# Query blocks first to last in a fused decoder trunk on one core

## The chip, the core and the metric

The kernel runs on one core of a Trainium2 chip, in one launch. The time is the device time of the whole program in microseconds (us), from the first to the last instruction with a little around it. A core has five engines, each with its own queue that it works through in order: TensorE (matmuls, PE in the profile, its weight loads PEld), VectorE (DVE), ScalarE (ACT), GpSimd (POOL) and SyncE (SP, which here only issues DMAs). They wait for each other by semaphores. Matmuls write to PSUM, eight banks of 128 partitions by 512 fp32 words.

## The reference

Two layers over 512 tokens of width 1024 in fp32. Each is a SwiGLU, a mixing part and a second SwiGLU, all with residuals. The mixing part, cut to what matters:

```python
h = rms_norm(x, mix_norm[l])
a, g, q, k, v = jnp.split(h @ w_in[l], splits, axis=-1)
conv_out = conv_module(a, g, conv_w[l], conv_b[l], conv_norm[l])      # 512 channels, 31 causal taps
...
def block(args):                       # 128 queries, 4 heads, 2 maps each, causal
    qi, i = args
    s = jnp.einsum("bhmqd,bhmkd->bhmqk", qi, k) * scale + bias[None, :, None]
    s = jnp.where((dist >= 0)[None, None, None], s, -1e30)
    p = jax.nn.softmax(s, axis=-1)
    a = p[:, :, 0] - lam * p[:, :, 1]
    return jnp.einsum("bhqk,bhkd->bhqd", a, v)
...
o = rms_norm(o, subln_g) * (1.0 - lam_init)
x = x + jnp.concatenate([conv_out, diff_out], axis=-1) @ w_out[l]
```

Query block i of four sees the keys of blocks 0 to i alone. The result of one block does not depend on another's, and the output projection adds up its two halves per token, so both may be taken in any order.

## The kernel before

Features lie on partitions and tokens along the row: `x`, and its split into a high part and a rest (`acth`, `actl`), are eight tiles of 128 x 512. To keep fp32 precision with faster matmuls most products are three: high by high, high by rest, rest by high (`mm3`, L200, L203, L204). Weights are split in the same way when they arrive (`parts_of`: ScalarE copies at L101, VectorE or GpSimd subtracts at L102). `chunk` loads two tiles of 128 x 512 from a ring of five and splits them.

The kernel is a Python program that emits instructions for a scheduler. The scheduler puts every engine's queue in an order of its own, from priorities in the program's order and its estimate of durations; where buffers are shared it adds semaphore waits. So a change of the program's order changes queues on all engines.

`mixer` does one mixing part. First come the projections: convolution inputs (`conv_in`, gate at L785 to L791 on VectorE), queries and keys (`project`, `to_features`), and four value tiles (`project_values`, L843 to L845: 24 matmuls of 512 columns each, evacuated by ScalarE at L846). They keep TensorE full while VectorE and GpSimd already do convolution taps: channel tile 0 is wholly on GpSimd (31 taps), 1 and 2 on VectorE, 3 shared (10 taps on GpSimd, L885, fed by ScalarE at L884; the other 21 on VectorE, L895 and L899, joined at L902).

Attention runs in 16 steps, a query block i with a head h. A step has two score maps of 128 x W, W = 128 (i + 1):

- `softmaxes`: two score matmuls (L930, fp32) into a bank of tag "sc" and one of tag "po", two banks each; for each map VectorE adds the bias and takes the row's minimum (L934; scores are negated), ScalarE the exponential with its sum (L938), the first map from an SBUF tile that L934 writes, the second in its bank; then VectorE inverts the sum (L941), scales it (L943) and joins both maps (L944). The "sc" bank is free after L934, the "po" bank after L944.
- `keys_first`, two steps later: i + 1 transposes of the joined map into the one bank "tp" (L951) and ScalarE's copy (L953).
- `values`, three steps later: i + 1 products with the values (L960) into a bank `ps_o`. After the last head of a block its norm follows: square on ScalarE (L969), sum on VectorE (L971), GpSimd adds and takes the inverse root (L972, L261 as `rs_y`), VectorE scales (L975).
- `block_out`, five steps later: four transposes (L987) and the split of the result (L989 on ScalarE, L990 on VectorE) into `acth`, `actl`.

`conv_finish` sums the squares of the convolution per token (TensorE transposes, L268; VectorE L272, L273; GpSimd `rs_y`; VectorE L288; TensorE `ps_spread`, L292; ScalarE L296), then scales and activates the four channel tiles (GpSimd L910, ScalarE L912, VectorE L913, ScalarE L914, VectorE L915).

The output projection makes three passes over eight feature tiles: the attention half of two query blocks (256 columns, 96 matmuls), the convolution half of all tokens (512 columns, 96 matmuls), the attention half of the other two blocks. Each pass loads and splits its weights again, on ScalarE and GpSimd. Its banks are "sc" and "po" again; VectorE adds each result to `x` (L1037), and in the last pass `after(m)` begins the preparation of the next SwiGLU.

Before, attention takes query block 3 first and block 0 last, and values are projected for tokens 384 to 511 first. The first pass of the output projection is that of tokens 256 to 511.

Of the kernel before, what the change touches and what calls it, by code (L numbers as in the profile page):

```python
# [20 lines left out]
SEQ = 512  # L21
DM = 1024
KT = DM // P
NT = SEQ // P
# [7 lines left out]
HEADS = 4  # L32
# [38 lines left out]
def trunk(ctx: ExitStack, tc: tile.TileContext, xt, par, lamv, relb, onehot,  # L71
# [17 lines left out]
    def bank(tag, name):  # L89
        return psum.tile([P, 512], F32, tag=tag, name=name, bufs=BANKS[tag])  # L90
# [14 lines left out]
    def chunk(src, eng=None):  # L105
        w = []
        for n in range(2):
            raw = ring("wraw")
            nc.sync.dma_start(raw, src[:, n * 512 : (n + 1) * 512])
            w.append(parts_of(raw, eng))  # L110
        return w

    def wpart(w, b, n=P):
        hi, lo = w[b * n // 512]
        c = b * n % 512
        return hi[:, c : c + n], lo[:, c : c + n]
# [81 lines left out]
    def mm3(ps, w, x, start, stop, pin=False):  # L198
        (wh, wl), (xh, xl) = w, x
        first = T.matmul(ps, wh, xh, start=start, stop=False)  # L200
        if pin:
            tc.keep_in_program_order(first)
        T.matmul(ps, wh, xl, start=False, stop=False)  # L203
        T.matmul(ps, wl, xh, start=False, stop=stop)  # L204
# [553 lines left out]
    def mixer(l, pr, after, begun):  # L758
        with tc.tile_pool(name="mix", bufs=1) as mp, tc.tile_pool(name="mt", bufs=2) as mt:
# [74 lines left out]
            def project_values(j):  # L834

                if 2 not in wts:
                    wts[2] = [chunk(wqkv[l, 2, kc], G) for kc in range(KT // 2)]
                t = slice(j * P, (j + 1) * P)
                ps = bank("mm", "ps_v")
                for k in range(KT):  # L840
                    wh, wl = wpart(wts[2][k // 2], k % 2, 512)
                    xh, xl = pr[k]
                    T.matmul(ps, xh[:, t], wh, start=k == 0, stop=False)  # L843
                    T.matmul(ps, xh[:, t], wl, start=False, stop=False)  # L844
                    T.matmul(ps, xl[:, t], wh, start=False, stop=k == KT - 1)  # L845
                S.activation(vv[:, j].rearrange("p h d -> p (h d)"), ps, AF.Copy, scale=row["c"][:, j : j + 1])  # L846
# [68 lines left out]
                    V.scalar_tensor_tensor(cl[:, c, :], z, hg, f32(ch[:, c, :]), op0=ALU.mult, op1=ALU.subtract)  # L915


            steps = [(i, h) for i in reversed(range(NT)) for h in range(HEADS)]
            sums, pos, maps, ats = {}, {}, {}, {}

            def softmaxes(i, h):
# [72 lines left out]
            def attend(n):  # L994
                if n < len(steps):
                    softmaxes(*steps[n])
                if 2 <= n < len(steps) + 2:
                    keys_first(*steps[n - 2])
                if 3 <= n < len(steps) + 3:
                    values(*steps[n - 3])  # L1000
                if n >= 5 and steps[n - 5][1] == HEADS - 1:
                    block_out(steps[n - 5][0])
# [12 lines left out]

            for n in range(2):
                attend(n)
                project_values(NT - 1 - 2 * n)
                project_values(NT - 2 - 2 * n)
            for c in range(CT):  # L1020
                conv_taps(c, POOL_TAPS[c])
            for n in range(2, len(steps) + 5):
                attend(n)
            conv_finish()

            for half, t in ((1, slice(SEQ // 2, SEQ)), (0, slice(0, SEQ)), (1, slice(0, SEQ // 2))):
                w = [None] * 4
                for m in range(KT):  # L1030
                    if w[m // 2] is None:
                        w[m // 2] = chunk(wout[l, half, m // 2], G)
                    ps = bank(("sc", "po")[m % 2], "ps_out")[:, : t.stop - t.start]
                    for kk in range(4):
                        k = half * 4 + kk
                        mm3(ps, wpart(w[m // 2], (m % 2) * 4 + kk), (ch[:, k, t], cl[:, k, t]), kk == 0, kk == 3)
                    V.tensor_tensor(x[:, m, t], ps, x[:, m, t], op=ALU.add)  # L1037

                    if half == 1 and t.start == 0 and m < KT // 2:
                        after(m)  # L1040
            for m in range(KT // 2, KT):
                after(m)
# [16 lines left out]
    for l in range(DEPTH):  # L1059
        nxt = {}  # L1060

        def preparing(gain, l2=l):
            def after(m):
                if m == 0:
                    nxt["p"] = Prep(l2, gain)
                nxt["p"].tile(m)
            return after

        def store(m):
            nc.sync.dma_start(out[m], x[:, m, :])  # L1070

        with tc.tile_pool(name="ffn", bufs=1) as fp:
            begun = ffn(fp, pr, gu1[l], dn1[l], preparing("mix_norm"), begun,
                        lambda tail: begin(nxt["p"], [[wag[l, c, i] for i in range(2)] for c in range(2)], tail),
                        (l == 0, 1), aside if l == 0 else None)
        mixer(l, nxt["p"], preparing("ffn2_norm"), begun)
        with tc.tile_pool(name="ffn", bufs=1) as fp:
            begun = begin(nxt["p"], [[gu2[l, m, i] for i in range(2)] for m in range(2)])
            if l + 1 < DEPTH:
                begun = ffn(fp, nxt["p"], gu2[l], dn2[l], preparing("ffn1_norm", l + 1), begun,  # L1080
                            lambda tail: begin(nxt["p"], [[gu1[l + 1, m, i] for i in range(2)] for m in range(2)], tail), (0, 1))
            else:
                ffn(fp, nxt["p"], gu2[l], dn2[l], store, begun, lambda tail: tail(), (0, 0))
        pr = nxt["p"]
# [74 lines left out]
```

## Time and profile before

| what | value |
|---|---|
| time, median of 3 runs | 1771.87 us (1771.71 to 1772.9) |
| time of the profiled execution | 1772.54 us |
| its span, first to last instruction | 1770.8 us |
| TensorE busy | 1759.9 us, 99% |
| weight loads busy | 1621.3 us, 92% |
| VectorE / ScalarE / GpSimd busy | 1470.9 / 1039.5 / 515.1 us |
| granted TensorE clock, mean | 1.000 |
| score matmuls, first to last in the program | 453.3 to 1379.1 us |

The profile is that of one execution. Where a row of a timeline reads `453.48 3.60 PE L930 MATMUL ps_sc<-kt,qz ... x8`, eight records of line 930 on TensorE begin at 453.48 us and take 3.60 us; the tile written stands left of the arrow, those read right of it. A group's row gives the count, the busy time with the mean duration of one in nanoseconds, and the idle time of the engine just before the group's instructions with what ended it. A window's row gives, for each engine, busy us and instructions in brackets, then the granted clock, the share of the DMA engines and GB/s. Matmuls overlap one another, so a busy TensorE is not one at its peak; the distance between the starts says more than the durations.

### The profile page before, as it was taken

To read this page: it belongs to the slowest core of one execution; us is meant where nothing else is said; L and a number is where in the kernel's file an instruction comes from. 1 tells how busy PE (TensorE), PEld (TensorE's weight loads), DVE (VectorE), ACT (ScalarE), POOL (GpSimd) and SP (SyncE) were. 2 spreads that over 40 slices of the span, in tenths; PEclk is the share of its full clock that TensorE was granted. 3 is DMA by queue.
4 is the path that set the end of the run, shared out by engine and by line. 5 is a ranking of instruction groups with operands and counts; after the bars stand their busy time and mean duration, and the time that the engine had idled before them with its cause. 6 is when DMAs were issued, how large, how long until landed. Compare 5 with 4: busy or idle time off the path is not lost.

```text
span 1770.8 us, 32986 instructions
## 1 busy us (share of the span) xinstructions
PE 1759.9 (99%) x11853; PEld 1621.3 (92%) x11853; DVE 1470.9 (83%) x2642; ACT 1039.5 (59%) x1951; POOL 515.1 (29%) x497
## 2 busy tenths in 40 slices
PE   9999999999999999999999999999999999999998
PEld 7799999988788899999988999999887888999998
DVE  7969888969877969889987798899698678698987
ACT  6546566755865436566644565666559554465664
POOL 1011112169970011112200121121798600111122
PEclk9999999999999999999999999999999999999999
DMA  7457677533223457687544577766231335577774
GB/s 222 135 135 184 166 197 190 135 122 96 71 78 113 123 130 178 172 198 177 143 144 108 149 176 180 194 161 177 81 113 48 101 105 134 133 184 173 194 176 126
DMA packets 165894, 257.79 MB, mean 146 GB/s; under 512 B 19191, under 2 KB 61958, under 8 KB 165728
## 3 DMA queue, kind: packets, MB, share of 16 engines
q1 hardware_dynamic: 129024, 201.38, 36.7%
q0 software_dynamic: 36416, 54.12, 19.0%
q8 instruction: 93, 1.52, 0.3%
q14 instruction: 73, 0.60, 0.1%
q10 hardware_dynamic: 288, 0.16, 0.0%
HBM read 253.48 MB, written 3.42 MB: 145 GB/s over the span
## 4 chain that ended last, share of the span: by engine, by line
PE 95%; DVE 2%; DMA 1%; POOL 1%; ACT 1%; issue 0%; SPq 0%; ACTq 0%; DVEq 0%; POOLq 0%
PE ps_pair L435 36%; PE ps_pair L524 17%; PE ps_pair L203 9%; PE ps_pair L204 9%; PE ps_pair L200 9%; PE ps_out L200 2%; PE ps_out L203 2%; PE ps_out L204 2%; PE ps_pair L815 2%; PE ps_pair L814 2%; PE ps_pair L813 2%; PE ps_sc L930 1%; PE ps_v L844 1%; PE ps_v L843 1%; PE ps_v L845 1%; POOL wlo L102 0%
## 5 line engine op out<-in xcount | busy, mean ns | idle before, releaser
L101 ACT ACTIVATE whi<-wraw 128x512 fp32r<-128x512 f32 x744 | 454.0, 628 | 421.9 <-PE ps_pair L203 174.8
L102 DVE TENSOR_TENSOR wlo<-wraw,whi 128x512 fp32r<-128x512 f32 x640 | 427.0, 685 | 116.7 <-ACT whi L101 105.2
L160 POOL DMA_DIRECT2D wsum<-in_gu x128 | 112.2, 907 | 703.7 <-DMA wsum<-in_gu 276.0
L435 PE MATMUL ps_pair<-acth,wlo 128*128 128x256 f32 x1024 | 289.8, 283 | 0.0
L435 PE MATMUL ps_pair<-actl,whi 128*128 128x256 f32 x1024 | 289.8, 283 | 0.0
L435 PE MATMUL ps_pair<-acth,whi 128*128 128x256 f32 x1024 | 289.8, 283 | 0.0
L435 PE MATMUL ps_pair<-th,whi 128*128 128x256 f32 x768 | 217.3, 283 | 0.0
L435 PE MATMUL ps_pair<-tl,whi 128*128 128x256 f32 x768 | 217.3, 283 | 0.0
L435 PE MATMUL ps_pair<-th,wlo 128*128 128x256 f32 x768 | 217.3, 283 | 0.0
L200 PE MATMUL ps_pair<-acth,whi 128*128 128x512 f32 x512 | 199.4, 394 | 0.5 <-ACT acth L309 0.4
L203 PE MATMUL ps_pair<-actl,whi 128*128 128x512 f32 x512 | 199.5, 390 | 0.3 <-DVE actl L310 0.3
L204 PE MATMUL ps_pair<-acth,wlo 128*128 128x512 f32 x512 | 199.2, 390 | 0.0
L435 PEld LDWEIGHTS ps_pair<-actl,whi 128*128 128x128 f32 x1024 | 196.6, 192 | 0.2
L435 PEld LDWEIGHTS ps_pair<-acth,whi 128*128 128x128 f32 x1024 | 196.6, 192 | 0.2
L435 PEld LDWEIGHTS ps_pair<-acth,wlo 128*128 128x128 f32 x1024 | 196.6, 192 | 0.0
L160 POOL DMA_DIRECT2D wsum<-in_dn x112 | 98.8, 1132 | 266.6 <-DMA wsum<-in_dn 45.6
L435 PEld LDWEIGHTS ps_pair<-th,whi 128*128 128x128 f32 x768 | 147.5, 192 | 0.0
L435 PEld LDWEIGHTS ps_pair<-tl,whi 128*128 128x128 f32 x768 | 147.5, 192 | 0.0
L435 PEld LDWEIGHTS ps_pair<-th,wlo 128*128 128x128 f32 x768 | 147.5, 192 | 0.0
L102 POOL TENSOR_TENSOR wlo<-wraw,whi 128x512 fp32r<-128x512 f32 x104 | 137.1, 1339 | 31.8 <-ACT whi L101 19.5
L524 PE MATMUL ps_pair<-hh,whi 128*128 128x256 f32 x512 | 144.9, 283 | 0.0
L524 PE MATMUL ps_pair<-hl,whi 128*128 128x256 f32 x512 | 144.9, 283 | 0.0
(207 smaller groups left out, 4445.2 us busy)
## 6 DMA issues: line engine op xcount, KB each, us to landing
wraw<-in_gu SPq DMA_DIRECT2D x284, 256.0 KB, 3.5
wsum<-in_gu SPq DMA_DIRECT2D x128, 256.0 KB, 3.8
wsum<-in_gu POOLq DMA_DIRECT2D x128, 256.0 KB, 4.7
wraw<-in_dn SPq DMA_DIRECT2D x68, 256.0 KB, 3.3
wraw<-in_wqkv SPq DMA_DIRECT2D x48, 256.0 KB, 2.9
wraw<-in_wout SPq DMA_DIRECT2D x48, 256.0 KB, 3.0
wraw<-in_dn SPq DMA_DIRECT2D x64, 128.0 KB, 4.2
wraw<-in_wag SPq DMA_DIRECT2D x32, 256.0 KB, 3.0
```

Source lines behind the costliest of these rows:

```text
L101: S.activation(hi, raw, AF.Copy)
L102: (eng or V).tensor_tensor(out=lo, in0=raw, in1=f32(hi), op=ALU.subtract)
L160: nc.gpsimd.dma_start(dst[:, to], src, accum_op=ALU.add)
L200: first = T.matmul(ps, wh, xh, start=start, stop=False)
L203: T.matmul(ps, wh, xl, start=False, stop=False)
L204: T.matmul(ps, wl, xh, start=False, stop=stop)
L435: mm = T.matmul(ps, l, r, start=first and i == j == 0, stop=False, skip_group_check=True)
L524: mm = T.matmul(ps, s[:, f], r, start=side not in self.begun, stop=False, skip_group_check=True)
L813: T.matmul(ps[n], xh[:, t], wh, start=k == 0, stop=False)
L814: T.matmul(ps[n], xh[:, t], wl, start=False, stop=False)
L815: T.matmul(ps[n], xl[:, t], wh, start=False, stop=k == KT - 1)
L843: T.matmul(ps, xh[:, t], wh, start=k == 0, stop=False)
```

## The change

Attention's 16 steps are listed with block 0 first. The value tiles follow the same order: tokens 0 to 127 first, two tiles behind each of the first two steps. The first pass of the output projection is the attention half of tokens 0 to 255, the third that of tokens 256 to 511; the next part's preparation stays with the third pass.

```diff
-            steps = [(i, h) for i in reversed(range(NT)) for h in range(HEADS)]
+            steps = [(i, h) for i in range(NT) for h in range(HEADS)]
...
             for n in range(2):
                 attend(n)
-                project_values(NT - 1 - 2 * n)
-                project_values(NT - 2 - 2 * n)
+                project_values(2 * n)
+                project_values(2 * n + 1)
...
-            for half, t in ((1, slice(SEQ // 2, SEQ)), (0, slice(0, SEQ)), (1, slice(0, SEQ // 2))):
+            for half, t in ((1, slice(0, SEQ // 2)), (0, slice(0, SEQ)), (1, slice(SEQ // 2, SEQ))):
...
-                    if half == 1 and t.start == 0 and m < KT // 2:
+                    if half == 1 and t.stop == SEQ and m < KT // 2:
                         after(m)
```

## The prediction

> **What bounds the kernel now.** I read the page's chain of waits first, then windows of the mixers, the timelines of TensorE and VectorE in the first attention, and the groups by shape there.
>
> ```profile
> PE 95%; DVE 2%; DMA 1%; POOL 1%; ACT 1%; issue 0%; SPq 0%; ACTq 0%; DVEq 0%; POOLq 0%
> ```
>
> TensorE sets the time: 95% of the chain that ended last is its own work. The change adds and removes no matmul, so it can only alter how long TensorE stands still in the two mixers. The windows cut the first mixer where the last value projection is issued (467.80) and where the conv statistics begin (492.66).
>
> ```profile
> core 0: us, PE busy (x) PEld busy (x) DVE busy (x) ACT busy (x) POOL busy (x), PEclk, DMA share, GB/s
> 467.80:492.66 24.86, 24.42 (x144) 18.44 (x143) 21.61 (x75) 24.12 (x68) 21.12 (x19) 1.00 0.29 85
> 492.66:506.66 14.00, 13.33 (x105) 12.20 (x104) 12.80 (x48) 11.01 (x34) 9.01 (x9) 1.00 0.01 2
> 506.66:520.00 13.34, 13.34 (x83) 11.88 (x82) 8.89 (x13) 7.67 (x14) 13.26 (x11) 1.00 0.48 142
> 1345.40:1370.10 24.70, 24.28 (x143) 18.27 (x142) 21.42 (x74) 23.94 (x68) 20.97 (x19) 1.00 0.29 86
> ```
>
> TensorE is nearly full here; ScalarE (24.12 of 24.86) and VectorE (21.61) have little room. Mixer 2 repeats mixer 1. What TensorE does per map comes from start times, since its durations overlap:
>
> ```profile
> 453.48 3.60 PE L930 MATMUL ps_sc<-kt,qz 128*128 128x512 f32 x8
> ...
> 467.80 1.88 PE L930 MATMUL ps_sc<-kt,qz 128*128 128x512 f32 x4
> 469.52 0.60 PE L951 MATMUL ps_at<-ident,e 128*128 128x128 f32 x4
> 469.95 2.53 PE L930 MATMUL ps_sc<-kt,qz 128*128 128x512 f32 x6
> ...
> 472.75 1.06 PE L960 MATMUL ps_o<-vv,at 128*128 128x128 f32 x8
> 473.65 2.75 PE L930 MATMUL ps_sc<-kt,qz 128*128 128x384 f32 x8
> 476.23 0.60 PE L951 MATMUL ps_at<-ident,e 128*128 128x128 f32 x4
> ...
> 491.23 0.70 PE L930 MATMUL ps_sc<-kt,qz 128*128 128x256 f32 x2 [0.40 <-DVE e L944]
> 491.77 0.38 PE L951 MATMUL ps_at<-ident,e 128*128 128x128 f32 x2
> ```
>
> A score matmul is two records. Four records at width 512 take 1.72 us, 0.86 a matmul; eight at 384 take 2.58, 0.645 each. So 256 is 0.43 and 128 is 0.215 by width. A transpose is 0.43/4 = 0.11; a value product, two records, 0.90/4 = 0.225. The released score at 491.23 took 0.54, not 0.43: after a stop 0.11 more goes by, in which its weights were not loaded ahead.
>
> The visible idle time understates the stops. The groups between 484.37 and 496.86 (12.49 us), the small maps' time:
>
> ```profile
> L960 PE MATMUL ps_o<-vv,at 128*128 128x128 f32 x32 | 4.8, 278 | 0.5 <-ACT at L953 0.5
> L930 PE MATMUL ps_sc<-kt,qz 128*128 128x256 f32 x10 | 3.3, 430 | 0.4 <-DVE e L944 0.4
> L951 PE MATMUL ps_at<-ident,e 128*128 128x128 f32 x14 | 2.6, 277 | 0.0
> L930 PE MATMUL ps_sc<-kt,qz 128*128 128x128 f32 x12 | 2.3, 286 | 0.0
> L987 PE MATMUL ps_o<-ident,ov 128*128 128x128 f32 x8 | 1.2, 272 | 0.0
> L268 PE MATMUL ps_rows<-ident,csum 128*128 128x128 f32 x4 | 0.6, 272 | 0.0
> ```
>
> At the prices above: 32 x 0.1125 + 10 x 0.215 + 26 x 0.11 + 12 x 0.108 = 9.9 us. So some **2.6 us a mixer** are lost now, all around the small maps. That is also the most that the change can win.
>
> **The change, part by part.** *The order of the blocks.* Widths now run 128, 256, 384, 512, and the compiled order follows. The first two steps' scores slip between the value projections; they were 4 x 0.86 us and are 4 x 0.215, so the projections end 2.6 us earlier, at about 465.2. From there to the statistics TensorE has: scores 4 at 128, 8 at 256, 8 at 384, 6 at 512 (14.6 us), 24 transposes (2.6), 21 value products (4.7), two blocks' output transposes and the statistics' (12 x 0.11 = 1.3). That is **23.3 us**. No output projection stands among it: its first matmul now comes right behind the statistics, since it needs block 1.
>
> VectorE's work for the same stretch:
>
> ```profile
> L934 DVE CUSTOM_DVE_ANT_0 e<-ps_sc,bias 128x512 f32<-128x512 f32 x4 | 2.8, 688 | 3.3 <-PE ps_sc L930 3.1
> L934 DVE CUSTOM_DVE_ANT_0 e<-ps_sc,bias 128x256 f32<-128x256 f32 x4 | 1.7, 421 | 0.0
> L934 DVE CUSTOM_DVE_ANT_0 e<-ps_sc,bias 128x128 f32<-128x128 f32 x4 | 1.1, 280 | 0.0
> L944 DVE SCALAR_TENSOR_TENSOR e<-ps_sc,c,e 128x512 f32<-128x512 f32 x4 | 3.0, 745 | 0.1
> L944 DVE SCALAR_TENSOR_TENSOR e<-ps_sc,c,e 128x128 f32<-128x128 f32 x4 | 1.4, 344 | 0.0
> L971 DVE TENSOR_REDUCE so<-sq 128x4 f32<-128x512 f32 x4 | 2.7, 677 | 0.0
> ```
> ```profile
> 454.53 0.69 DVE L934 CUSTOM_DVE_ANT_0 e<-ps_sc,bias 128x512 f32<-128x512 f32 x1 [2.44 <-PE ps_sc L930]
> ...
> 475.09 0.16 DVE L941 RECIPROCAL r<-sums 128x1 f32<-128x1 f32 x1
> 475.28 0.27 DVE L943 TENSOR_SCALAR c<-r,nlam,sums 128x1 f32<-128x1 f32 x1
> 475.59 0.75 DVE L944 SCALAR_TENSOR_TENSOR e<-ps_sc,c,e 128x512 f32<-128x512 f32 x1
> 476.26 0.56 DVE L934 CUSTOM_DVE_ANT_0 ps_sc<-ps_sc,bias 128x384 f32<-128x384 f32 x1
> ...
> 490.70 0.47 DVE L944 SCALAR_TENSOR_TENSOR e<-ps_sc,c,e 128x256 f32<-128x256 f32 x1
> ```
>
> An operation starts 0.08 before the one ahead ends (475.59 + 0.75 - 476.26); L934 at 384 takes 0.56, L944 at 256 0.47 and at 384, between its neighbours, 0.61. The slots are so 0.61, 0.48, 0.34, 0.20 for a map's L934, twice a step, 0.67, 0.53, 0.40, 0.27 for L944, and up to 0.50 (475.09 to 475.59) for L941 with L943; where others stand between, I take 0.40. Twenty-six L934 in the stretch (4, 8, 8 and 6 by width) give 11.0 us, eleven L944 4.9, eleven pairs 4.4. Two blocks' ends, the conv sum (L902) and the last two taps are nine operations of some 0.63 (row L971 less 0.08): 5.7. Together **26.0 us**, starting 0.4 behind TensorE. So TensorE cannot do its 23.3 in under 26.4: at least 3.1 us of stops. A step at width 128 is 0.77 us of TensorE against 1.1 of VectorE, at 512 3.0 against 2.4; before, the wide maps came first and TensorE was the slower, and by the small ones it had output matmuls.
>
> The two score banks of each kind tie the engines tighter than sums do: a score two steps on waits for L934 (first map) or L944 (second map) of the step that has its bank, and everything behind it on TensorE waits too. I followed the compiled order instruction by instruction at these slots, with 0.2 us from TensorE to VectorE (the first score issued by 453.48 + 0.86, read at 454.53), 0.06 back (L944 ends at 491.17, the score starts at 491.23), ScalarE's and GpSimd's queues beside it. Stops, in block and head: 0.1 before the score of (1,1), 0.8 (1,2), 0.1 and 0.0 second maps of (1,0) and (1,2), 0.7 first score of block 2, 0.7 (2,1), 0.2 (1,3), 0.5 and 0.05 transposes behind ScalarE's copy, 0.1 a value product, 1.1 the score of (3,2), behind two block ends on VectorE, 0.3 (3,3). Sum **4.7 us**; with 0.11 for weights at ten of them **5.8**. Bounds: 3.1 (the floor) and 7.8 (GpSimd, below).
>
> *The output projection's order.* No matmul, load or split is added; SyncE's and the weights' order stays, so the DMAs count nothing. The attention half of tokens 0 to 255 (96 matmuls) now lies beside block 3, which covers its stops; before, the second half's lay beside block 0. I leave 0.4 us of stops there; 0 and 1.3 bound it (half of today's 2.6). The conv half starts when 96 matmuls are issued in both kernels; the conv scaling starts late with the statistics, and so does TensorE: nothing. Block 3's end has the conv half as cover (the window from 506.66, full); without it VectorE's and GpSimd's part alone (L971, rs_y and two operations of L971's size) would cost some 3 us.
>
> *The sum*: 5.8 + 0.4 - 2.6 = **+3.6 us a mixer, +7.2 in all**. The profiled execution's span of 1770.8 becomes 1778.0; it was timed at 1772.54, 0.67 above the median, so I put the sum on the median: 1771.87 + 7.2 = **1779.1 us**.
>
> **The rivals.** *Only the floor is paid.* VectorE's idle time before L934 in its row (3.1 us behind TensorE) shows that it is often ready first. Then stops are 3.1 + 0.4, +0.9 a mixer: 1773.7 us, no measurable change.
>
> *Faster: the output matmuls cover everything.* They go beside the widest block, and the head has only four 128-wide steps. If VectorE is so far ahead at 465.2 that the narrow maps do not hold TensorE, only 0.4 is left of the 2.6: 1771.87 - 4.4 = 1767.5. It decides where the head's stops stay under 0.8 us; the floor of 3.1 speaks against it.
>
> *More: GpSimd late.* Its queue is in order, and the compiled one puts the block's rs_y behind conv adds:
>
> ```profile
> 486.14 1.02 POOL L261 TENSOR_TENSOR rs_y<-so,mhalf 128x4 f32<-128x4 f32 x1
> 487.13 1.28 POOL L885 TENSOR_TENSOR yp<-yp,prod 128x512 f32<-128x512 f32 x1
> ```
>
> The statistics stand on TensorE ahead of all output matmuls and need the last add and the sum of squares. In my walk they are ready 1.1 us early; with two adds more (2 x 1.26) ahead of them TensorE stands 1.5 to 2 us: +3 to 4 in all, 1782.7 us.
>
> *The granted clock falls.* All windows show 1.00. If stops grew into one that halves the clock for the window from 492.66, its 13.3 busy us would double: 1771.87 + 2 x (3.6 + 13.3) = 1806 us. My longest stop is 1.1 us. [...]
>
> That the change does not do what it says is out: the compiled order has both reversals.
>
> **How the numbers follow.** Forecast 0.66, with its own range 1774.5 to 1783 (floor plus loads; GpSimd a little late); floor only 0.18; faster 0.06; GpSimd 0.09; clock 0.01. About 0.2% (3.5 us) is what a measurement of this kernel tells from no change, so the line is 1775.4: of the forecast's share 0.04 lies under it. Slower 0.62 + 0.09 + 0.01 = 0.72, same 0.22, faster 0.06. The range 1772.5 to 1785 leaves out the faster case, the clock and the outer parts of the others.
>
> **What would show it.** From the last value matmul to the statistics: 27.5 to 28.5 us (24.9 before), then output matmuls almost without stops. TensorE's waits there name L934 and L944 for some 4 us a mixer; VectorE busy 95% of it. Everything outside 441 to 525 and its like in mixer 2 keeps its length. The prediction is wrong if that stretch stays under 26 us, if TensorE waits for GpSimd's csum, or if stops show in the conv half.

## The result, and the profile after

| | before | after |
|---|---|---|
| median of ten runs | 1772.11 us (1771.53 to 1772.9) | 1777.01 us (1775.69 to 1780.11) |
| ratio after to before | | 1.0027, 95% interval 1.0019 to 1.0035 |
| profiled execution | 1772.54 us, span 1770.8 | 1780.11 us, span 1778.3 |

The changed kernel is 4.9 us slower. Its profiled execution is the slowest of its ten, so the spans differ by more, 7.5 us; where the surplus lies is said below.

The first mixer is read from TensorE's timeline: its first value matmul, its last output matmul, and between them the matmuls behind its visible stops (in the changed kernel with the matmul ahead of each). The columns are start, duration, engine, line, operation, how many records, and in brackets the idle time just before with its releaser. First the kernel before, with the second of its two visible stops (the first, at 491.23, stands in the prediction):

```profile
441.70 0.39 PE L843 MATMUL ps_v<-whi,acth 128*128 128x512 f32 x1
...
494.94 0.71 PE L960 MATMUL ps_o<-vv,at 128*128 128x128 f32 x4 [0.53 <-ACT at L953]
...
545.66 0.28 PE L204 MATMUL ps_out<-acth,wlo 128*128 128x256 f32 x1
```

Then the changed kernel:

```profile
440.97 0.39 PE L843 MATMUL ps_v<-whi,acth 128*128 128x512 f32 x1
...
464.35 0.39 PE L845 MATMUL ps_v<-whi,actl 128*128 128x512 f32 x1
...
466.44 0.70 PE L930 MATMUL ps_sc<-kt,qz 128*128 128x256 f32 x2
467.66 0.70 PE L930 MATMUL ps_sc<-kt,qz 128*128 128x256 f32 x2 [0.51 <-DVE mn L934]
...
469.07 0.60 PE L930 MATMUL ps_sc<-kt,qz 128*128 128x256 f32 x2
470.32 1.34 PE L930 MATMUL ps_sc<-kt,qz 128*128 128x384 f32 x4 [0.65 <-DVE mn L934]
...
471.61 0.39 PE L960 MATMUL ps_o<-vv,at 128*128 128x128 f32 x2
472.53 0.91 PE L930 MATMUL ps_sc<-kt,qz 128*128 128x384 f32 x2 [0.54 <-DVE mn L934]
...
483.48 0.81 PE L930 MATMUL ps_sc<-kt,qz 128*128 128x384 f32 x2
485.18 1.13 PE L930 MATMUL ps_sc<-kt,qz 128*128 128x512 f32 x2 [0.89 <-DVE mn L934]
...
492.54 0.60 PE L268 MATMUL ps_rows<-ident,csum 128*128 128x128 f32 x4
...
547.17 0.28 PE L204 MATMUL ps_out<-acth,wlo 128*128 128x256 f32 x1
```

From the first value matmul to the last output matmul the mixer took 545.66 - 441.70 = 103.96 us before and 547.17 - 440.97 = 106.20 after: **+2.2 us**. The second mixer shows the same (1319.1 to 1423.1 against 1321.4 to 1427.6). Together they are 4.4 of the 4.9 us. The two old stops are gone, and four new ones stand at scores that VectorE's L934 releases.

The windows of the same three parts, with the middle part of the second mixer (busy time and instructions of TensorE, its weight loads, VectorE, ScalarE and GpSimd, then granted clock and DMA):

```profile
440.97:464.58 23.61, 23.61 (x114) 19.74 (x113) 20.46 (x41) 16.87 (x34) 21.02 (x18) 1.00 0.15 48
464.58:492.54 27.96, 25.24 (x127) 16.74 (x126) 24.55 (x90) 26.26 (x80) 24.65 (x23) 1.00 0.22 74
492.54:547.17 54.63, 54.63 (x361) 49.19 (x360) 39.45 (x70) 32.62 (x61) 29.73 (x24) 1.00 0.30 97
...
1345.00:1372.90 27.90, 25.16 (x127) 16.67 (x126) 24.50 (x90) 26.26 (x80) 24.64 (x22) 1.00 0.22 75
```

The stretch from the last value projection to the conv statistics is 27.96 us (24.86 before), and after it TensorE has no visible gap. In the stretch ScalarE is the fullest helper: 26.26 of 27.96 us, 94%, where VectorE has 24.55, 88%. Who waits for whom in that window (total, times, longest):

```profile
PEld ps_sc L930 <- DVE mn L934: 4.9, 6, 1.5
PE ps_sc L930 <- DVE mn L934: 2.6, 4, 0.9
DVE ps_sc L934 <- PE ps_sc L930: 1.9, 3, 1.2
...
DVE e L934 <- PE ps_sc L930: 0.8, 1, 0.8
```

The wait goes both ways: TensorE stands for L934, and L934 stands 2.7 us for scores. Not all of that is one circle. The longest, 1.2 us, is for a score that lies behind the one standing until 470.32, and it delays the L934 for which TensorE then stands until 472.53. But 0.8 us is for the first score of the stretch, behind the last value matmul, and at the other two TensorE had not stopped, it was still busy with work ahead of the score.

The profiled execution's other 3 us lie in the last SwiGLU, at the end of the program. TensorE's timeline there, before and after, and ScalarE's after:

```profile
1751.76 0.39 PE L524 MATMUL ps_pair<-yh,whi 128*128 128x256 f32 x1 [0.46 <-ACT keep L557]
```
```profile
1757.68 0.38 PE L524 MATMUL ps_pair<-yh,whi 128*128 128x256 f32 x1 [1.90 <-ACT keep L557]
```
```profile
1754.95 0.63 ACT L101 ACTIVATE whi<-wsum 128x512 fp32r<-128x512 f32 x1 [5.56 <-DMA wsum<-in_dn]
```

ScalarE waited for a weight chunk that landed late in that execution, and TensorE's stop was 1.90 us instead of 0.46; about 1.6 us more were lost behind it, where the granted clock fell to 0.50 (last section). The scatter of the changed kernel's runs, 4.4 us against 1.4, fits such a chance wait, which is not shown for the other runs; the median is read with the mixers.

### The profile page after: what moved, and what is told of

The parts are those of the page before. It is cut to its first block, busy times and chain, and to the rows that moved or that the text cites. A ratio compares the mean times of both kernels' runs of the same rounds, so it can differ in the third digit from the quotient of the medians.

```text
span 1778.3 us, 32994 instructions
## 1 busy us (share of the span) xinstructions
PE 1762.5 (99%) x11853; PEld 1621.5 (91%) x11853; DVE 1472.9 (83%) x2642; ACT 1036.7 (58%) x1951; POOL 514.3 (29%) x497
## 4 chain that ended last, share of the span: by engine, by line
PE 93%; DMA 2%; DVE 2%; ACT 1%; issue 1%; POOL 0%; SPq 0%; DVEq 0%; ACTq 0%; POOLq 0%
PE ps_pair L435 36%; PE ps_pair L524 15%; PE ps_pair L203 9%; PE ps_pair L204 9%; PE ps_pair L200 9%; PE ps_out L200 2%; PE ps_out L204 2%; PE ps_out L203 2%; PE ps_pair L813 2%; PE ps_pair L815 2%; PE ps_pair L814 2%; PE ps_sc L930 2%; DMA wraw<-in_dn 1%; PE ps_o L960 1%; PE ps_v L845 1%; PE ps_v L844 1%
## 5 line engine op out<-in xcount | busy, mean ns | idle before, releaser
L102 DVE TENSOR_TENSOR wlo<-wraw,whi 128x512 fp32r<-128x512 f32 x640 | 426.9, 685 | 114.5 <-ACT whi L101 103.2
L102 DVE TENSOR_TENSOR wlo<-wsum,whi 128x512 fp32r<-128x512 f32 x192 | 130.0, 683 | 23.3 <-ACT whi L101 23.1
L102 POOL TENSOR_TENSOR wlo<-wraw,whi 128x512 fp32r<-128x512 f32 x104 | 137.4, 1337 | 38.6 <-ACT whi L101 24.5
```

The lines of the kernel that those rows point to most:

```text
L102: (eng or V).tensor_tensor(out=lo, in0=raw, in1=f32(hi), op=ALU.subtract)
```

## The experiments

Twelve kernels ran. Theory A is the prediction's sum: VectorE has more work in the stretch than TensorE. The others were formed on the way: B, each score pays for handing its bank over; C, the order of the queues of TensorE and VectorE alone; D, ScalarE's load. "Mixer" is the first one, from first value matmul to last output matmul as above.

| run | what it is | median, us | ratio to before (95%) | mixer, us |
|---|---|---|---|---|
| e1_passes_back | after, passes as before | 1802.06 | 1.0162 (1.0148 to 1.0176) | 117.91 |
| e2_passes_only | before, passes as after | 1798.46 | 1.0141 (1.0125 to 1.0157) | 116.21 |
| e3_values_only | before, values first to last | 1773.50 | 1.0001 (0.9992 to 1.0009) | 103.99 |
| e4_mixed | blocks in pairs, wide beside narrow | 1784.33 | 1.0061 (1.0048 to 1.0073) | 109.19 |
| e5_map_in_sbuf | after, second map in SBUF | 1779.69 | 1.0042 (1.0030 to 1.0055) | 106.89 |
| e6_before_sbuf | before, second map in SBUF | 1778.98 | 1.0036 (1.0023 to 1.0050) | 107.11 |
| e7_no_rest | after, less VectorE work | 1776.50 | 1.0021 (1.0012 to 1.0030) | 105.80 |
| e8_pairs_1032 | after, blocks 1, 0, 3, 2 | 1779.35 | 1.0035 (1.0022 to 1.0047) | 106.94 |
| e9_spread | after, values spread over 4 steps | 1776.00 | 1.0021 (1.0013 to 1.0030) | 105.68 |
| e10_spread6 | after, values spread over 6 steps | 1776.69 | 1.0026 (1.0016 to 1.0037) | 106.29 |
| e11_no_prod | after, less ScalarE work | 1774.57 | 1.0010 (1.0001 to 1.0018) | 104.62 |
| e12_before_no_prod | before, less ScalarE work | 1774.41 | 1.0011 (1.0002 to 1.0020) | 104.47 |

The ratio is taken against runs of the kernel before on the same chip, so it can differ a little from one against the median in the first table.

### Which part of the change does it

```diff
 e1, on the kernel after
-            for half, t in ((1, slice(0, SEQ // 2)), (0, slice(0, SEQ)), (1, slice(SEQ // 2, SEQ))):
+            for half, t in ((1, slice(SEQ // 2, SEQ)), (0, slice(0, SEQ)), (1, slice(0, SEQ // 2))):
...
-                    if half == 1 and t.stop == SEQ and m < KT // 2:
+                    if half == 1 and t.start == 0 and m < KT // 2:
 e2, on the kernel before: the same two lines, the other way round
 e3, on the kernel before
-                project_values(NT - 1 - 2 * n)
-                project_values(NT - 2 - 2 * n)
+                project_values(2 * n)
+                project_values(2 * n + 1)
```

> The changed kernel, but the output projection's passes as before (attention half of tokens 256 to 511 first). Theory A (the output matmuls fill TensorE's stops only if the first pass needs the blocks that finish early): the first pass now has to wait for the end of block 3 and nothing stands beside that block, so TensorE stands still for 4 to 8 us a mixer more after the conv statistics: 1785 to 1793 us. The stretch from the last value projection to the statistics stays at 27.5 to 28.5 us. Rival (the passes' order matters little, since TensorE is full either way): 1776 to 1778 us.

> The kernel before with the passes' order of the change alone (tokens 0 to 255 first), blocks still last to first. Theory A: the first pass waits for block 0, the last, and the narrow blocks lose their filler: 6 to 9 us a mixer, 1784 to 1790 us. Rival (the passes' order matters little): 1771 to 1773 us.

> The kernel before with only the value projections first to last. Both theories: all four tiles are projected before the first map needs a value, so nothing: 1771.4 to 1772.6 us. A rival in which the order of the values carries part of the loss would show 1773.5 or more.

The order of the values costs nothing that can be seen. The median of e3, 1773.50 us, lies just on the rival's mark, but the kernel before had 1772.49 on the same chip with runs up to 1774.59, the ratio's interval holds 1, and the mixer is as long as before. The passes must follow the blocks, as theory A had it, but each mismatch cost far more than the 4 to 9 us a mixer that were expected: the mixer is 117.91 - 106.20 = 11.7 us longer than that of after (e1), and 116.21 - 103.96 = 12.2 longer than that of before (e2). TensorE's timeline and the windows of e1 say why:

```profile
511.32 1.08 PE L987 MATMUL ps_o<-ident,ov 128*128 128x128 f32 x4 [5.04 <-DVE ov L975]
```
```profile
505.00:510.00 5.00, 1.29 (x11) 1.05 (x9) 4.01 (x6) 3.23 (x6) 3.05 (x4) 0.90 0.00 0
...
514.00:516.00 2.00, 2.00 (x11) 2.00 (x11) 0.57 (x1) 0.00 (x0) 0.00 (x0) 0.50 0.00 0
...
518.00:520.00 2.00, 2.00 (x14) 2.00 (x13) 0.42 (x1) 0.63 (x1) 0.93 (x2) 0.68 0.16 41
```

With the first pass needing the last block, TensorE stood 5.04 us in one piece for the block's end, and while it stood the granted clock (the figure before the DMA share) fell to 0.50; it came back only at about 519, and in between a full TensorE began 11 matmul records from 514 to 516, at 0.50, against 19 from 520 to 522, at 1.00. The visible stops behind the statistics are 7.0 us in all, inside what was expected of e1. Most of the other 4.7 us is the clock: an estimate is half of the 8 us from 511.3 to 519.3. That is the prediction's rival of the clock. In e2 the clock fell too, and there before the longest stop:

```profile
502.00:503.00 1.00, 0.51 (x2) 0.51 (x3) 0.96 (x3) 0.44 (x2) 1.00 (x2) 0.72 0.00 0
```
```profile
507.42 1.11 PE L987 MATMUL ps_o<-ident,ov 128*128 128x128 f32 x4 [2.70 <-DVE ov L975]
```

It was 1.00 up to 502 and 0.50 from 503 to 516. Ahead of the fall stood three stops of 0.80, 0.37 and 0.78 us close together (up to 500.19, 501.16 and 502.49), none of them over a microsecond; the 2.70 us came after it.

### Is it the sum of VectorE's work?

```diff
 e7, on the kernel after
-                V.scalar_tensor_tensor(
-                    cl[:, CT:, tq], pt, gsub[l], f32(ch[:, CT:, tq]), op0=ALU.mult, op1=ALU.subtract
-                )
+                if i > 1:
+                    V.scalar_tensor_tensor(
+                        cl[:, CT:, tq], pt, gsub[l], f32(ch[:, CT:, tq]), op0=ALU.mult, op1=ALU.subtract
+                    )
 e8, on the kernel after
-            steps = [(i, h) for i in range(NT) for h in range(HEADS)]
+            steps = [(i, h) for i in (1, 0, 3, 2) for h in range(HEADS)]
 e4, on the kernel before (and the passes on tokens of blocks 0 and 3, then 1 and 2)
-            steps = [(i, h) for i in reversed(range(NT)) for h in range(HEADS)]
+            steps = [(i, h) for pair in ((3, 0), (2, 1)) for h in range(HEADS) for i in pair]
```

> The changed kernel without VectorE's L990 for blocks 0 and 1 (the small parts of these blocks' attention output are left out), which takes 0.67 us of VectorE twice in the stretch. Theory A: each microsecond taken off VectorE there is a microsecond less of stops: stretch shorter by 1.2 to 1.4 us a mixer, time about 1774.4 (1773.8 to 1775.2). Rival B: only the score of block 3, head 2, that stands behind the block ends gets earlier, by 0.7 us a mixer: 1775.3 to 1776.2.

> The changed kernel with the blocks in the order 1, 0, 3, 2. Theory A: per step TensorE has 1.53, 0.77, 3.06, 2.3 us and VectorE 1.53, 1.1, 2.3, 1.9; only block 0's four steps and the conv sum are VectorE's, the wide block comes third and lets VectorE catch up: some 1 to 1.5 us a mixer of stops less than the changed kernel, 1773.5 to 1775.5 us. Rival B (stops are paid at each bank handed over, whatever the order): as the changed kernel, 1776.3 to 1777.7.

> The kernel before with blocks taken in pairs, head by head: (3,0) (0,0) (3,1) (0,1) and so on, then blocks 2 and 1; the first pass of the output projection takes the tokens of blocks 3 and 0, the third those of 1 and 2. By theory A a wide and a narrow step together are 3.8 us of TensorE against 3.5 of VectorE, so no stretch is bound by VectorE, and most of the 2.6 us of stops that the kernel before has in each mixer can go as well: 1767 to 1771 us. Rival B (each score waits for the bank of the step ahead, whatever the sums): narrow scores wait behind wide ones, 1772 to 1776 us.

Theory A falls in all three, and the time ranges of rival B are missed too. In e7 two operations (1.35 us of VectorE a mixer) are gone, and the mixer is 0.4 us shorter; the interval of its ratio overlaps that of after. TensorE's stops are the same four, to 0.02 us:

```profile
468.52 0.70 PE L930 MATMUL ps_sc<-kt,qz 128*128 128x256 f32 x2 [0.52 <-DVE mn L934]
...
471.20 1.13 PE L930 MATMUL ps_sc<-kt,qz 128*128 128x384 f32 x3 [0.67 <-DVE mn L934]
...
473.42 0.91 PE L930 MATMUL ps_sc<-kt,qz 128*128 128x384 f32 x2 [0.54 <-DVE mn L934]
...
486.07 1.13 PE L930 MATMUL ps_sc<-kt,qz 128*128 128x512 f32 x2 [0.89 <-DVE mn L934]
```

Rival B of that run had the last of them 0.7 shorter. VectorE's timeline of after shows the chain into it:

```profile
483.36 0.57 DVE L934 CUSTOM_DVE_ANT_0 ps_sc<-ps_sc,bias 128x384 f32<-128x384 f32 x1 [0.41 <-PE ps_sc L930]
...
483.84 0.68 DVE L971 TENSOR_REDUCE so<-sq 128x4 f32<-128x512 f32 x1
484.44 0.68 DVE L934 CUSTOM_DVE_ANT_0 e<-ps_sc,bias 128x512 f32<-128x512 f32 x1
...
485.05 0.74 DVE L990 SCALAR_TENSOR_TENSOR actl<-ps_o,gsub,acth 128x512 fp32r<-128x512 f32 x1
```

The L934 that frees the bank for 485.18 starts at 484.44. Ahead of it VectorE was idle for 0.41 us, waiting for a score that stood later in TensorE's queue; then it did one L934 and the block's L971, and only then the one that TensorE needed. L990 comes behind it: taking it away could not help there. By the step sums of their expectations the two engines are better balanced in e4 and e8 than in after; e4 is slower than after by more than both intervals, and e8 is no faster, its mixer 0.7 us longer. So VectorE's sum does not set the time of this stretch. At the last stop it is the order in the queues that does. At the first, the L934 that TensorE needs (467.18) comes behind two taps of the convolution on a VectorE that has had no gap since 465.00; the second and third are taken up with ScalarE below and with the waits above. For e4 and e8 no such chain is shown.

### Adding work to VectorE

```diff
 e5, on the kernel after; e6, on the kernel before
+                e1 = mt.tile([P, SEQ], F32, tag="e1", name="e1", bufs=2)[:, :W]
...
-                for m, (sc, e) in enumerate(zip(scs, (e0, scs[1]))):
+                for m, (sc, e) in enumerate(zip(scs, (e0, e1))):
...
-                V.scalar_tensor_tensor(e0, scs[1], c2, e0, op0=ALU.mult, op1=ALU.add)
+                V.scalar_tensor_tensor(e0, e1, c2, e0, op0=ALU.mult, op1=ALU.add)
```

> The changed kernel, with the second map's biased scores and exponentials written to a tile of their own in SBUF, so that its score bank is free after L934 and not after L944. Theory A (TensorE waits because VectorE has more work in the stretch than TensorE): the work is the same, so the stops stay, some move from L944 to L934: stretch 27.4 to 28.4 us, time 1776.3 to 1777.7. Rival B (the latency of handing two banks to and fro makes the stops): the waits for L944 go and the later ones shrink, stretch 26.3 to 27.2 us, time 1773.5 to 1775.5.

> The kernel before with the second map in a tile of its own in SBUF, as in the run on the changed kernel. Theory A: TensorE's few stops there are mostly for ScalarE's copies, and VectorE's work is the same: 1771.2 to 1772.6 us. Rival B: the waits for L944 (0.8 us in all) go: 1770 to 1771.2 us.

Both were slower, which neither theory had. The groups of this operation at width 384 (busy, mean ns of one), in the kernel before and in e6, where the added line makes it L945:

```profile
L944 DVE SCALAR_TENSOR_TENSOR e<-ps_sc,c,e 128x384 f32<-128x384 f32 x4 | 2.5, 614 | 0.0
```
```profile
L945 DVE SCALAR_TENSOR_TENSOR e<-e,c,e 128x384 f32<-128x384 f32 x4 | 4.5, 1125 | 0.1
```

With both inputs in SBUF the combination took 1.13 us on average there, instead of 0.61. Over all 16 steps of the first mixer it takes 4.7 us more of VectorE in e6, and the mixer is 107.11 - 103.96 = 3.15 us longer; in e5 it takes 5.4 us more, and the mixer is 106.89 - 106.20 = 0.7 us longer. Again the sum of VectorE's work does not tell the time: the same kind of work costs much or little by where it falls. The runs thus measure a price and do not test the hand-over of the banks; that stayed untested.

### Covering the hand-over, and taking load off ScalarE

```diff
 e9, on the kernel after (e10: one behind steps 0, 2 and 4, the last behind step 5)
-            for n in range(2):
+            for n in range(4):
                 attend(n)
-                project_values(2 * n)
-                project_values(2 * n + 1)
+                project_values(n)
...
-            for n in range(2, len(steps) + 5):
+            for n in range(4, len(steps) + 5):
 e11, on the kernel after; e12, on the kernel before
-                        p = mt.tile([P, SEQ], F32, tag="prod", name="prod")
-                        S.activation(p, us[c][:, t : t + SEQ], AF.Copy, scale=pars[l][:, wc + t : wc + t + 1])
-                        G.tensor_tensor(yp, yp, p, op=ALU.add)
+                        G.tensor_tensor(yp, yp, us[c][:, t : t + SEQ], op=ALU.add)
```

> The changed kernel with one value projection behind each of the first four steps, instead of two behind each of the first two. Theory C (from the run without L990: the stops are made by order, TensorE's queue standing at a score for L934 of two steps before, while VectorE waits for a score behind it; 1.35 us less of VectorE's work gave only 0.4): with projection matmuls between the narrow scores the hand-over is covered, the stops of block 0 and of the first steps of block 1 go, 1 to 2 us a mixer: 1773 to 1775 us. Rival (the projections and the value products share the mm banks, so a projection now waits for a bank that a block's output holds): nothing or a loss, 1776.5 to 1780 us.

> The changed kernel with a value projection behind every second of the first six steps and the last behind the sixth. Theory C: block 0 and two steps of block 1 lie beside projections, so more is covered than with four steps: 1 to 2.5 us a mixer, 1772 to 1775 us. Rival (the shared mm banks): 1776.5 to 1781 us, and more than with four steps.

Theory C's gain did not come: e9 is 0.5 us a mixer shorter than after, e10 is level with it. The time of e10 lies in its rival's range, but not for the rival's reason: in neither run does a value projection of the first mixer wait for a bank. In e9 the stop before (1,2) is gone, and the four stops of 0.51 to 0.89 us have become six of 0.19 to 0.37, 1.6 us in all in place of 2.6. Two of them on TensorE's timeline, and a row of who waits for whom in the stretch:

```profile
470.91 1.39 PE L930 MATMUL ps_sc<-kt,qz 128*128 128x384 f32 x3 [0.30 <-DVE mn L934]
...
477.10 0.91 PE L930 MATMUL ps_sc<-kt,qz 128*128 128x384 f32 x2 [0.26 <-DVE e L944]
```
```profile
DVE r L941 <- ACT ps_sc L938: 1.5, 3, 0.9
```

VectorE now waits 1.5 us for ScalarE's exponentials, where in after it is 0.4. ScalarE's timeline of after has no gap from 464.4 to 477.4; a piece of it, and the one operation of VectorE in the stretch that waits for an exponential:

```profile
467.09 0.71 ACT L884 ACTIVATE prod<-u,par 128x512 f32<-128x512 f32 x1
...
468.25 0.62 ACT L101 ACTIVATE whi<-wraw 128x512 fp32r<-128x512 f32 x1
468.77 0.32 ACT L938 ACTIVATE ps_sc<-ps_sc,mn 128x128 f32<-128x128 f32 x1
```
```profile
469.25 0.16 DVE L941 RECIPROCAL r<-sums 128x1 f32<-128x1 f32 x1 [0.43 <-ACT ps_sc L938]
```

Ahead of the second exponential of (0,3) stand a product of the conv and a weight split, for which no score waits. VectorE stood 0.43 us for it, and the L934 that ends TensorE's stop at 470.32 is behind that in VectorE's queue. This is the whole of what the trace of after shows of ScalarE holding VectorE; in the kernel before the same wait is 1.5 us in its stretch. The group of the conv products (L884) in the stretch:

```profile
L884 ACT ACTIVATE prod<-u,par 128x512 f32<-128x512 f32 x7 | 5.1, 722 | 0.8 <-POOL yp L885 0.8
```

> The changed kernel without ScalarE's products of the conv taps (L884): GpSimd adds the inputs as they are, so these taps' weights are left out. VectorE's and GpSimd's work is the same; ScalarE, whose timeline after the last value projection shows no gap for 13 us, loses some seven operations of 0.72 us in the stretch, 5 us of its 26.3. Theory D (ScalarE is what keeps the score banks: its exponentials queue behind work that no score waits for, and VectorE's queue waits for them): the stretch falls to about 24.5 to 26 us, the time to 1769 to 1774 us. Theory C (order between TensorE and VectorE alone): the stretch stays above 27 us, 1775.8 to 1777.5 us.

> The kernel before with the same products left out. There ScalarE is busy for 24.1 of 24.9 us of the stretch, but wide maps come first. Theory D: some of the 2.6 us of stops a mixer go, 1768.5 to 1771 us. Theory C: 1771.5 to 1772.6 us. The difference between this run and the run on the changed kernel is what the order costs without ScalarE's load: by theory D under 2 us, by theory C still 4 to 5.

The window of the stretch in e11, and TensorE's only visible stops in it (two lines are gone, so L930 is L928 here):

```profile
464.89:491.25 26.36, 25.41 (x127) 16.49 (x126) 23.93 (x88) 22.51 (x72) 21.39 (x21) 1.00 0.23 69
```
```profile
468.55 1.13 PE L928 MATMUL ps_sc<-kt,qz 128*128 128x256 f32 x4 [0.33 <-DVE mn L932]
...
473.27 0.70 PE L928 MATMUL ps_sc<-kt,qz 128*128 128x256 f32 x2 [0.19 <-DVE e L942]
...
486.33 1.60 PE L958 MATMUL ps_o<-vv,at 128*128 128x128 f32 x12 [0.43 <-DVE actl L988]
```

The stretch fell by 1.6 us and the visible stops from 2.6 to 0.95, with the same maps on VectorE. The two orders then take 1774.57 and 1774.41 us and their mixers 104.62 and 104.47: the 4.9 us between them are 0.2. That is theory D's second number. Its first was half right: the changed kernel gained 1.6 us a mixer, just short of the range expected, but the kernel before lost 0.5 instead of gaining. TensorE's timeline of e12 has a new stop:

```profile
492.55 0.49 PE L928 MATMUL ps_sc<-kt,qz 128*128 128x128 f32 x2 [1.27 <-DVE e L942]
```

With the products gone the compiled order is another one in both kernels, and GpSimd no longer waits for them, so the two runs change load and order together. What is shown is that without the products the changed kernel loses 1.6 us a mixer less, and that VectorE waits for no exponential in that stretch. That ScalarE's load is part of what the new order pays for fits this, but is not shown apart from the reshuffled order; how much of the 0.5 us and of the 1.6 belongs to which stays open. None of the twelve beats the kernel before.

## Why the prediction was right, point by point

The forecast was 1779.1 us, slower; 1777.0 was measured.

- *TensorE alone counts, in the two mixers.* Right: 4.4 of the 4.9 us are there, in equal parts.
- *"27.5 to 28.5 us".* The stretch is 27.96 and 27.90, but that number is partly luck. It is the 23.3 us of TensorE's own work plus the 4.7 of stops. The 23.3 hold the four transposes of the statistics, 0.4 us, which begin where the stretch ends, and the number leaves out the 1.1 us of weight loads that the sum counts. TensorE's own work in the stretch is 22.9 us, so 5.1 are lost in it, where the sum has 5.8.
- *The named stops.* Right in place, and nearly in size. The largest four stand where they were put, at (1,2), the first score of block 2, (2,1) and (3,2). The idle times in brackets, 0.51 to 0.89, are short of the stops, as the prediction warned. From start to start, less the price of what stood ahead (467.66 - 466.44 - 0.43 for the first), they are 0.8, 0.8, 0.7 and 1.1 us; they were put at 0.8, 0.7, 0.7 and 1.1. All four wait for L934; L944 shows only among the waits of the weight loads, which are 4.9 us for L934 and 0.7 for L944.
- *The mis-sized terms* are the small ones in "with 0.11 for weights at ten of them 5.8", and "I leave 0.4 us of stops there". The four large stops with a load each were put at 3.7 and are 3.8 us. The small stops and the other loads were put at 2.1 and are 1.3. After the statistics no stop shows, and the old one at 494.94 is gone. So it is 5.1 - 2.6 = 2.5 us a mixer in place of 3.6; 2.2 were measured, and the 0.3 between them is not resolved at these prices.
- *"VectorE's work for the same stretch ... 26.0", and "VectorE busy 95% of it".* Wrong: 24.55 us of 27.96, 88%. Of the 26 operations of L934 24 stand in the stretch; the other two, at width 512 (1.2 us), come behind it. For the nine operations 0.63 was taken where L971's row less 0.08 is 0.60. The floor of 3.1 us is by the same sum 24.55 + 0.4 - 22.9 = 2.1. The walk held because it followed the queues, not because of this sum; e4, e7 and e8 show that the sum is no guide here. Nor did the narrow maps of the kernel before have output matmuls to cover them: the first stands at 496.86, behind the 2.6 us of stops.
- *The output projection's order.* Right in sign and reason: the filler must need the blocks that finish first. With the passes turned back e1 pays 11.7 us a mixer, part of it by the clock.
- *The conv half, and GpSimd.* Right: no stop in the conv half, and no wait of TensorE for csum. The GpSimd rival did not come.
- *The clock.* 1.00 in all mixer windows of the changed kernel, whose longest stop is 0.89 us; e1 and e2 show that the rival was real: the clock fell to 0.50 in e1 within a stop of 5.04 us, in e2 already behind three of 0.37 to 0.80 us close together. At which stop it falls no trace of before showed, so the 0.01 given to the rival was the author's estimate.
- *The faster case* needed the head's stops under 0.8 us. The three of them are 0.51 + 0.65 + 0.54 = 1.7 in visible idle time alone, and no output matmul lies beside the narrow blocks.

## What to carry to other kernels

When two orders have the same work, walk the compiled order through each engine's queue and the banks; sums of busy time did not forecast the time here, and two orders with better sums were no faster. Put the pass that needs the blocks finished first beside the blocks still running: the filler was worth more here than the order of the blocks, also because the clock fell from 1.00 to 0.50 around the stops of e1 and e2. Measure a stop from start to start: the four visible idle times of 0.51 to 0.89 us were stops of 0.7 to 1.1. Look which helper engine is fullest in the stretch itself, and what stands in its queue between the operations that free a bank.

## What the hardware showed unexpectedly

The clock fell behind a single stop well below the 5.04 us of e1. In the changed kernel's profiled execution, after the 1.90 us stop at the end of the program, the windows show:

```profile
1757.00:1758.00 1.00, 0.32 (x2) 0.32 (x3) 1.00 (x3) 0.62 (x2) 0.00 (x0) 1.00 0.00 0
...
1759.00:1760.00 1.00, 1.00 (x7) 1.00 (x6) 1.00 (x3) 0.34 (x1) 0.00 (x0) 0.50 0.00 0
...
1763.00:1764.00 1.00, 1.00 (x11) 1.00 (x10) 0.82 (x2) 0.00 (x0) 0.00 (x0) 1.00 0.50 199
```

TensorE restarted at 1757.68 at full clock and dropped to 0.50 about a microsecond later, for some 3.5 us. A stop of 1.27 us in e12 was followed by no drop: the clock was 1.00 in all windows from 489.58 to 548. So in these runs the clock fell behind one stop of 1.90 us, and in e2 behind stops of 0.80, 0.37 and 0.78 us close together, but not behind one of 1.27; no run shows a limit.

VectorE's combination of two SBUF tiles took longer beside GpSimd's 512-wide subtracts of weights (L102). Two of the same width in e6, 1.64 us and 0.62:

```profile
478.40 1.64 DVE L945 SCALAR_TENSOR_TENSOR e<-e,c,e 128x384 f32<-128x384 f32 x1
...
484.29 0.62 DVE L945 SCALAR_TENSOR_TENSOR e<-e,c,e 128x384 f32<-128x384 f32 x1
```

The first ran during three such subtracts (476.69 to 481.18), the second behind the last of them, which started at 479.6. The three took 4.49 us together, 3.75 in the kernel before, so GpSimd was slower there too. In the kernel before, with one input in PSUM, VectorE's operation took 0.61 us beside the same subtracts (at 478.94), and 0.61 to 0.62 in all four of this width. In the first mixer of e6 the combination took 4.7 us more of VectorE. That the two slowed together is measured here; the cause is not shown.
